# Eight blocks of an up projection made in two parts of the token columns

## Chip, cores and metric

The kernel runs on one core of a Trainium2 chip. Times are device microseconds of one execution; the time before is the median of two runs, 1305.54 us (1305.24 and 1305.84).

## What is computed

The reference is two transformer blocks over 256 tokens of width 1024, in float32. The first block mixes tokens (a gated branch and a banded attention) and then goes through a layer of 16384 experts, each with one up row and one down row. Every token picks 16 experts for each of 8 heads:

```python
q = (xb @ w_query).reshape(PEER_TOKEN_BLOCK, PEER_HEADS, 2, PEER_HALF)
...
g = jax.nn.softmax(best, axis=-1)
u = jnp.take(expert_u, eidx, axis=0)
h = jax.nn.gelu(jnp.einsum('thkd,td->thk', u, xb))
vv = jnp.take(expert_v, eidx, axis=0)
return jnp.einsum('thk,thkd->td', (g * h.astype(jnp.float32)).astype(xb.dtype), vv)
```

The second block has three mixers, gates, and a feed-forward layer of width 2816. The change concerns the product with `expert_u` only.

## The kernel before

The kernel doesn't gather experts. `experts` (L681) computes the up projection of all 16384 experts for all 256 tokens as 128 dense blocks of 128 experts, applies GELU, multiplies by a dense matrix of gates that is zero where a token didn't pick an expert, and computes the dense down projection in 128 blocks. The routing that makes the gates runs beside this on VectorE.

Every large product is made in three matmuls of the type float32r: each operand is held as a high part and a low part, and `mm3` (L179) adds high x high (L180), high weight x low (L181) and low weight x high (L182) into PSUM. The trace writes both float32r and plain float32 as f32. `project` (L187) does so for the 8 slices of the width 1024, so one block of the up projection is 24 matmuls of 128 rows by 256 token columns, with the 128 x 128 weight slices as the stationary operand; each matmul has its own weight load (LDWEIGHTS, the engine PEld in the trace). The token operands are the tiles `nh` and `nl`, the weights `wh` and `wl`:

```python
for k in range(n):
    wh, wl = self.cols(w, o + k)
    self.mm3(ps, wh, wl, xh[:, k0 + k, :], xl[:, k0 + k, :], k == 0, k == n - 1)
```

Weights come by DMA on SyncE's queue into `raw` (L166); ScalarE copies the high part (L171) and VectorE subtracts to make the low part (L116). Three blocks of weights are held ready at a time, and `ahead` (L104) starts the load of a later block when a buffer comes free.

The loop over the up blocks is at L754. Two blocks share one PSUM bank, `ps` (256 columns each), and after each odd block ScalarE applies GELU to both (L771). At i = 2, 22, 42 and 62 the loop first issues `short` (L257): four small f16 matmuls (L261). After each block `side.step` (L767) issues a share of VectorE's routing work: top-16 searches, one-hots and gates. The order of instructions on every engine is the order in which the program issues them.

Other lines that the text speaks of: L708 are plain float32 matmuls of 128 columns (the key scores of the routing); L229 are plain float32 matmuls of one column (mean squares for a norm); L846 and L870 are plain float32 matmuls of 256 columns; L669 are f16 matmuls of 64 columns (gates); L255 are matmuls on zeros of 128 columns, in plain float32, which the program issues at its start and later where TensorE would be idle.

Of the kernel before, what the change touches and what calls it, by code (L numbers as in the profile page):

```python
# [13 lines left out]
S = 256  # L14
# [41 lines left out]
class Prog:  # L56
# [624 lines left out]
    def experts(self):  # L681
        nc, tc, a, c = self.nc, self.tc, self.a, self.c
        with tc.tile_pool(name="sg", bufs=1) as sg:
# [19 lines left out]
            def scores(hp, qt):  # L703
                nonlocal pss
                if hp % 4 == 0:
                    pss = [self.bank("g").rearrange("p (h c) -> p h c", h=4) for _ in range(2)]
                for t in range(2):
                    self.mm(pss[t][:, hp % 4, :], qt[:, t * P:(t + 1) * P], sk[:, hp, :], start=True, stop=True)  # L708
                if hp % 4 == 3:
                    for t in range(2):  # L710
                        self.act(sc[t][:, hp - 3:hp + 1, :], pss[t], AF.Copy)
                    ready[0] += 1
# [3 lines left out]
            for hp in range(16):  # L716
# [6 lines left out]
                if hp < 2:  # L723
                    ps = first[hp]
                else:
                    ps = self.bank()[:, 0:S]
# [27 lines left out]
            for i in range(P):  # L754
                if i == 64:
                    side.rate = self.RATE[1]
                if i % 2 == 0:
                    ps = self.bank().rearrange("p (e t) -> p e t", e=2)
                if i in (2, 22, 42, 62):
                    self.short(iot)  # L760
                self.project(ps[:, i % 2, :], self.take(), self.nh, self.nl)
                while prev:
                    scores(*prev.pop(0))
                if i == P - 1:
                    side.rest()
                    self.hidden(hb0, hb1, 0)
                side.step()  # L767
                self.ahead()
                if i % 2:
                    o = self.up_order[i - 1]  # L770
                    self.act(hb0[:, o:o + 2, :] if i < 64 else hb1[:, o - 64:o - 62, :], ps, AF.Gelu_apprx_tanh)  # L771
# [38 lines left out]
            for i in range(P - 2):  # L810
# [4 lines left out]
                w = self.take()  # L815
# [26 lines left out]
            ps = self.pair()[:, 0, :].rearrange("p (e t) -> p e t", e=2)  # L842
            for j in range(2):
                w = self.take()
# [483 lines left out]
```

## Time and profile before

| what | value |
|---|---|
| median of two runs | 1305.54 us |
| the profiled execution | 1305.5 us |
| its span, first to last instruction | 1303.7 us |
| TensorE busy | 1291.5 us, 11518 matmuls |
| weight loads busy | 1256.1 us, 11518 loads |
| VectorE busy | 945.8 us |
| ScalarE busy | 673.0 us |
| granted TensorE clock | 0.999 of full speed |

Busy time counts each instruction from start to end, overlaps once. Matmuls overlap one another, so the pace of a run of matmuls is read from the starts, or from a run's length and count: (length - duration of the last) / (count - 1).

### The profile page before, as it was taken

To read this page: it belongs to the slowest core of one execution; us is meant where nothing else is said; L and a number is where in the kernel's file an instruction comes from. 1 tells how busy PE (TensorE), PEld (TensorE's weight loads), DVE (VectorE), ACT (ScalarE), POOL (GpSimd) and SP (SyncE) were. 2 spreads that over 40 slices of the span, in tenths; PEclk is the share of its full clock that TensorE was granted. 3 is DMA by queue.
4 is the path that set the end of the run, shared out by engine and by line. 5 is a ranking of instruction groups with operands and counts; after the bars stand their busy time and mean duration, and the time that the engine had idled before them with its cause. 6 is when DMAs were issued, how large, how long until landed. Compare 5 with 4: busy or idle time off the path is not lost.

```text
span 1303.7 us, 27324 instructions
## 1 busy us (share of the span) xinstructions
PE 1291.5 (99%) x11518; PEld 1256.1 (96%) x11518; DVE 945.8 (73%) x1517; ACT 673.0 (52%) x935; POOL 1.6 (0%) x9
## 2 busy tenths in 40 slices
PE   9999999999999999999999999999999999999998
PEld 8799999999999999999999999999999999999986
DVE  5567899878888887799985665556567576776743
ACT  7575454454544444444444554444677646655542
POOL 0000000000000000000000000000000000000000
PEclk9999999999999999999999999999999999999999
DMA  8545466655655555555556755564644456455652
GB/s 273 188 128 179 162 196 197 196 191 193 190 184 176 170 173 176 182 173 170 175 165 194 257 186 193 192 194 149 228 147 147 147 193 217 160 189 193 194 186 74
DMA packets 65211, 237.14 MB, mean 182 GB/s; under 512 B 7360, under 2 KB 7488, under 8 KB 64576
## 3 DMA queue, kind: packets, MB, share of 16 engines
q1 hardware_dynamic: 64800, 233.30, 54.8%
q10 hardware_dynamic: 288, 2.10, 0.5%
q8 instruction: 90, 1.47, 0.4%
q14 instruction: 33, 0.27, 0.1%
HBM read 233.27 MB, written 2.10 MB: 181 GB/s over the span
## 4 chain that ended last, share of the span: by engine, by line
PE 94%; DVE 3%; ACT 2%; issue 1%; DMA 1%; SPq 0%; DVEq 0%; ACTq 0%
PE u L180 20%; PE u L181 19%; PE u L182 19%; PE g L180 7%; PE g L181 7%; PE g L182 7%; PE y L180 3%; PE y L182 3%; PE y L181 3%; PE y L669 2%; DVE wl L116 1%; ACT wh L171 1%; PE y L870 1%; DMA raw<-w_in_t 1%; PE y L846 1%
## 5 line engine op out<-in xcount | busy, mean ns | idle before, releaser
L116 DVE TENSOR_TENSOR wl<-raw,wh 128x1024 fp32r<-128x1024 f32 x426 | 519.1, 1222 | 271.4 <-ACT wh L171 270.7
L171 ACT ACTIVATE wh<-raw 128x1024 fp32r<-128x1024 f32 x426 | 451.1, 1060 | 485.5 <-PE u L181 376.6
L180 PE MATMUL u<-nh,wh 128*128 128x256 f32 x2176 | 609.6, 280 | 0.2 <-ACT big L1017 0.2
L181 PE MATMUL u<-nl,wh 128*128 128x256 f32 x2176 | 602.4, 277 | 0.9 <-DVE nl L733 0.5
L182 PE MATMUL u<-nh,wl 128*128 128x256 f32 x2176 | 601.7, 277 | 0.7 <-DVE wl L116 0.7
L180 PEld LDWEIGHTS u<-nh,wh 128*128 128x128 f32 x2176 | 408.7, 188 | 2.8 <-issue 1.7
L181 PEld LDWEIGHTS u<-nl,wh 128*128 128x128 f32 x2176 | 408.9, 188 | 2.0 <-DVE nl L272 0.7
L182 PEld LDWEIGHTS u<-nh,wl 128*128 128x128 f32 x2176 | 408.5, 188 | 1.0 <-DVE wl L116 0.9
L180 PE MATMUL g<-nh,wh 128*128 128x256 f32 x680 | 188.2, 277 | 0.0
L182 PE MATMUL g<-nh,wl 128*128 128x256 f32 x680 | 187.8, 276 | 0.0
L181 PE MATMUL g<-nl,wh 128*128 128x256 f32 x680 | 187.8, 276 | 0.0
L180 PEld LDWEIGHTS g<-nh,wh 128*128 128x128 f32 x680 | 127.6, 188 | 0.3 <-issue 0.3
L182 PEld LDWEIGHTS g<-nh,wl 128*128 128x128 f32 x680 | 127.7, 188 | 0.0
L181 PEld LDWEIGHTS g<-nl,wh 128*128 128x128 f32 x680 | 127.7, 188 | 0.0
L658 DVE TENSOR_TENSOR og<-ob,gT 128x1024 f16<-128x1024 f16 x64 | 41.4, 688 | 1.1
L654 DVE TENSOR_TENSOR oa<-iot,i1T 128x2048 f16<-128x2048 f16 x32 | 39.0, 1218 | 0.0
L669 PE MATMUL y<-og,oa 128*128 128x64 f16 x1024 | 35.4, 193 | 0.0
L669 PEld LDWEIGHTS <-oa 128*128 128x128 f16 x1024 | 31.6, 98 | 1.1
L1017 ACT ACTIVATE big<-u 128x256 f32<-128x256 f32 x30 | 11.5, 383 | 27.2 <-PE u L182 27.2
L181 PE MATMUL y<-brl,wh 128*128 128x256 f32 x80 | 22.4, 280 | 0.0
L180 PE MATMUL y<-brh,wh 128*128 128x256 f32 x80 | 22.3, 279 | 0.0
L182 PE MATMUL y<-brh,wl 128*128 128x256 f32 x80 | 22.3, 279 | 0.0
(342 smaller groups left out, 1388.8 us busy)
## 6 DMA issues: line engine op xcount, KB each, us to landing
raw<-peer_u SPq DMA_DIRECT2D x128, 512.0 KB, 3.6
raw<-peer_v SPq DMA_DIRECT2D x128, 512.0 KB, 3.6
raw<-w_in_t SPq DMA_DIRECT2D x50, 512.0 KB, 3.9
raw<-ffn_in SPq DMA_DIRECT2D x44, 512.0 KB, 4.0
raw<-ffn_out SPq DMA_DIRECT2D x22, 512.0 KB, 3.5
raw<-w_out SPq DMA_DIRECT2D x16, 512.0 KB, 3.6
raw<-w_query SPq DMA_DIRECT2D x16, 512.0 KB, 3.5
raw<-w_in_v SPq DMA_DIRECT2D x12, 512.0 KB, 4.4
```

The lines of the kernel that those rows point to most:

```text
L116: self.tt(out=lo, in0=raw, in1=h.bitcast(F32), op=ALU.subtract)
L171: self.act(h, raw, AF.Copy)
L180: self.mm(ps, wh, xh, start=start, stop=False, **kw)
L181: self.mm(ps, wh, xl, start=False, stop=False, **kw)
L182: self.mm(ps, wl, xh, start=False, stop=stop, **kw)
L654: tt(out=split(oa), in0=row(0, P), in1=runs(i1T[:, d], P), op=ALU.is_equal)
L658: tt(out=split(og[:, s]), in0=split(ob), in1=runs(gT[:, s, d], 64), op=ALU.mult)
L669: nc.tensor.matmul(ps[:, j, :], oa[:, j, :], og[:, s, j, :], start=(s == 0), stop=(s == 1))
L846: self.mm(ps[:, j, :], w[:, k * P:(k + 1) * P], self.mem[:, k, :], start=(k == 0), stop=(k == KD - 1))
L870: mm(pss[:, t, 0:256], self.mem[:, 4 * i + k, t * P:(t + 1) * P], w[:, k * 256:(k + 1) * 256], start=(4 * i + k == 0), stop=(4 * i + k == ...
L1017: copy = lambda v, scale=1.0: lambda ps: act(v, ps, AF.Copy, scale=scale)
```

## The change

For i // 2 = 4, 5, 6 and 7 (blocks 8 to 15) the block's product is made in two calls of `project`, over the columns n to 256 and then over 0 to n, with n = 32, 48, 64 and 128. All other blocks have n = 0 and one call over 256 columns, as before.

```diff
-                self.project(ps[:, i % 2, :], self.take(), self.nh, self.nl)
+                n = {4: 32, 5: 48, 6: 64, 7: 128}.get(i // 2, 0)
+                w = self.take()
+                for o, m in ((n, S), (0, n)):
+                    if o < m:
+                        self.project(ps[:, i % 2, o:m], w, self.nh[:, :, o:m], self.nl[:, :, o:m])
```

On TensorE, where block 7 ends and block 8 begins, the order before is this (`u_2134` is the PSUM bank of blocks 6 and 7, `u_2206` that of 8 and 9; `wh_2129` and `wl_2130` are the weights of block 8):

```order
L180 MATMUL u_2134<-nh_74,wh_2094 128x256
L181 MATMUL u_2134<-nl_75,wh_2094 128x256
L182 MATMUL u_2134<-nh_74,wl_2095 128x256
L180 MATMUL u_2206<-nh_74,wh_2129 128x256
L181 MATMUL u_2206<-nl_75,wh_2129 128x256
L182 MATMUL u_2206<-nh_74,wl_2130 128x256
```

Now the same place reads so:

```order
L180 MATMUL u_2134<-nh_74,wh_2094 128x256
L181 MATMUL u_2134<-nl_75,wh_2094 128x256
L182 MATMUL u_2134<-nh_74,wl_2095 128x256
L180 MATMUL u_2206<-nh_74,wh_2129 128x224
L181 MATMUL u_2206<-nl_75,wh_2129 128x224
L182 MATMUL u_2206<-nh_74,wl_2130 128x224
```

The matmuls of block 8 have 224 columns instead of 256.

On TensorE 24 matmuls further, before, block 8 ends and block 9 (weights `wh_2166`, `wl_2167`) begins:

```order
L180 MATMUL u_2206<-nh_74,wh_2129 128x256
L181 MATMUL u_2206<-nl_75,wh_2129 128x256
L182 MATMUL u_2206<-nh_74,wl_2130 128x256
L180 MATMUL u_2206<-nh_74,wh_2166 128x256
L181 MATMUL u_2206<-nl_75,wh_2166 128x256
L182 MATMUL u_2206<-nh_74,wl_2167 128x256
```

Now block 8 goes on there with its second part:

```order
L180 MATMUL u_2206<-nh_74,wh_2129 128x224
L181 MATMUL u_2206<-nl_75,wh_2129 128x224
L182 MATMUL u_2206<-nh_74,wl_2130 128x224
L180 MATMUL u_2206<-nh_74,wh_2129 128x32
L181 MATMUL u_2206<-nl_75,wh_2129 128x32
L182 MATMUL u_2206<-nh_74,wl_2130 128x32
```

The 24 matmuls of 32 columns use the weights of block 8 a second time, in the same sequence; block 9 comes 24 matmuls later. TensorE has 192 matmuls more in all, and the other engines have the instructions that they had, in the same order.

## Rows read from the trace of the kernel before

**Rows 1.** The page: busy time by engine, and the chain by engine.
```profile
span 1303.7 us, 27324 instructions
PE 1291.5 (99%) x11518; PEld 1256.1 (96%) x11518; DVE 945.8 (73%) x1517; ACT 673.0 (52%) x935; POOL 1.6 (0%) x9
...
PE 94%; DVE 3%; ACT 2%; issue 1%; DMA 1%; SPq 0%; DVEq 0%; ACTq 0%
```

**Rows 2.** Timeline of PE around the short matmuls: start, length, engine, line, form, count.
```profile
171.80 0.29 PE L261 MATMUL y<-iot 128*128 128x64 f16 x4
171.92 0.36 PE L180 MATMUL u<-nh,wh 128*128 128x256 f32 x1
172.12 0.29 PE L181 MATMUL u<-nl,wh 128*128 128x256 f32 x1
...
226.43 0.29 PE L261 MATMUL y<-iot 128*128 128x64 f16 x4
226.56 0.36 PE L180 MATMUL u<-nh,wh 128*128 128x256 f32 x1
```

**Rows 3.** Windows: length, busy time of each engine, granted clock, DMA.
```profile
1.00:5.00 4.00, 3.98 (x19) 3.98 (x20) 0.71 (x2) 2.12 (x4) 0.00 (x0) 1.00 0.79 227
...
188.28:210.08 21.80, 21.80 (x195) 21.80 (x194) 21.21 (x75) 10.44 (x12) 0.00 (x0) 1.00 0.65 211
```

**Rows 4.** The chain in the window 188.28 to 210.08, by line.
```profile
by line: PE u L180 34.0%; PE u L181 33.7%; PE u L182 33.2%
```

**Rows 5.** Timeline of PE in the up blocks, first and last of 42 steps.
```profile
190.05 0.28 PE L180 MATMUL u<-nh,wh 128*128 128x256 f32 x1
190.16 0.28 PE L181 MATMUL u<-nl,wh 128*128 128x256 f32 x1
...
194.81 0.28 PE L180 MATMUL u<-nh,wh 128*128 128x256 f32 x1
```

**Rows 6.** Groups of instructions from 188 to 211 us: count, busy time, mean ns.
```profile
L180 PE MATMUL u<-nh,wh 128*128 128x256 f32 x68 | 18.8, 276 | 0.0
L180 PEld LDWEIGHTS u<-nh,wh 128*128 128x128 f32 x68 | 12.8, 188 | 0.0
```

**Rows 7.** L229 (ns min/median/max) and the timeline around it; L846's durations.
```profile
L229 PEld LDWEIGHTS y<-cst,big x28: 186/192/192, 124.4 to 1132.7; 128*128 128x128 f32 x28
L229 PE MATMUL y<-cst,big x28: 164/250/271, 124.4 to 1132.8; 128*128 128x1 f32 x28
...
904.09 1.37 PE L229 MATMUL y<-cst,big 128*128 128x1 f32 x11
...
900.50 3.61 PE L846 MATMUL y<-big,raw 128*128 128x256 f32 x16
903.95 1.84 PE L229 MATMUL y<-cst,big 128*128 128x1 f32 x16
905.66 3.70 PE L846 MATMUL y<-big,raw 128*128 128x256 f32 x16
...
L846 PE MATMUL y<-big,raw x32: 377/379/463, 900.5 to 909.0; 128*128 128x256 f32 x32
```

**Rows 8.** L708: its durations, and 12 of them in the timeline.
```profile
L708 PE MATMUL g<-hb x64: 270/275/275, 123.6 to 168.9; 128*128 128x128 f32 x64
...
167.71 1.50 PE L708 MATMUL g<-hb 128*128 128x128 f32 x12
```

**Rows 9.** L669: its durations, and 32 of them in the timeline.
```profile
L669 PEld LDWEIGHTS <-oa x1024: 95/98/101, 374.7 to 680.4; 128*128 128x128 f16 x171
L669 PE MATMUL y<-og,oa x1024: 193/193/203, 374.7 to 680.4; 128*128 128x64 f16 x171
...
374.72 1.11 PE L669 MATMUL y<-og,oa 128*128 128x64 f16 x32
```

**Rows 10.** Timeline of float32r matmuls of 512 columns.
```profile
56.42 0.40 PE L180 MATMUL u<-wh,nh 128*128 128x512 f32 x1
...
57.35 0.40 PE L181 MATMUL u<-wl,nh 128*128 128x512 f32 x1
```

**Rows 11.** Timeline of the last block of queries, first and last of 14 steps.
```profile
165.24 0.28 PE L180 MATMUL u<-nh,wh 128*128 128x256 f32 x1
...
166.89 0.28 PE L182 MATMUL u<-nh,wl 128*128 128x256 f32 x1
```

**Rows 12.** Timeline of the first matmuls of the run.
```profile
1.02 3.99 PE L255 MATMUL u<-zeros 128*128 128x128 f32 x17 [1.02 <-POOL zeros L248]
```

## Prediction

> **What bounds the kernel now.** I read the page first. TensorE is busy 1291.5 of 1303.7 us, and the chain that ended last is 94% PE [rows 1], so a stretch in which TensorE is slower moves the end, unless another engine waits there. Next comes the stretch that the change touches. The short matmuls at i = 2 and i = 22 place it: the first matmul behind them starts at 171.92 and 226.56, with 20 blocks and one more group of four short ones (0.13 us) between [rows 2]. That is (54.64 - 0.13) / 20 = 2.726 us a block, so blocks 8 to 15 stand from 171.92 + 6 x 2.726 = 188.28 to 210.08. In that window TensorE and its weight loads are busy for all of 21.80 us, VectorE for 21.21 [rows 3], and the chain runs through PE alone [rows 4]. VectorE is nearly full, but nothing there waits for it, and since the change only lengthens TensorE's part, VectorE gets more room.
>
> Then the pace of one matmul. A duration in the list (276 ns) overlaps the next one, so I take starts. From 190.05 to 194.81 there are 14 groups of three, 42 steps in 4.76 us: 113.3 ns for 256 columns [rows 5]. The weight loads keep the same pace, and their record of 188 ns shows the same overlap [rows 6]. So two things could set this pace, the 256 columns or the load of a 128x128 fp32 weight, and the change separates them: it halves the columns of a matmul on average and doubles the loads.
>
> **What the change removes and adds.** An up block is 8 x 3 = 24 matmuls. Eight blocks lose 192 matmuls of 256 columns: 192 x 113.3 ns = 21.75 us, which is the window of 21.80. They get 384 matmuls, each with its own load, since all 24 of the first part run before the second part begins and the weights change at each step. The number of columns is the same.
>
> What does a matmul cost that has few columns and a load of 128x128 fp32 weights? The trace has three witnesses. One column: 11 matmuls of the mean-square in 1.37 us, the last lasting 0.250, so (1.37 - 0.25) / 10 = 112.0 ns a step [rows 7]. 128 columns of plain fp32: 12 in 1.50 us, the last 0.275, so 111.4 [rows 8]. Against them 64 columns of f16: 32 in 1.11 us, the last 0.193, so 29.6 ns, and there the load is of f16 weights, with a record of 98 ns where the fp32 one has 188 to 192 [rows 6, 7, 9]. One column and 128 take the same time, and a change of the weights' type changes it: the load of fp32 weights sets some 112 ns, whatever the columns. I take 111.7, the mean of the two. The loads of the up projection are float32r, and they have the shape and the record length of the plain fp32 ones.
>
> Added: 384 x 111.7 = 42.89 us. Net: 42.89 - 21.75 = +21.1 us. By this all eight blocks come out alike, at 24 x 2 x 111.7 = 5.36 us in place of 2.72, whether cut 224 + 32 or 128 + 128.
>
> Bounds of this term. From below: a wide part could be paced by its columns if its load hid better than here. 512 columns step at (57.35 - 56.42) / 4 = 232.5 ns [rows 10], so a column costs (232.5 - 113.3) / 256 = 0.466 ns, and 224, 208 and 192 columns would take 98.4, 90.9 and 83.5. With the small part at 111.7 the pairs cost 96.8, 89.3 and 81.9 more than 113.3, and 128 + 128 costs 110.1 more: 48 of each make 18.2 us. From above: the same 256-column matmul also runs at (166.89 - 165.24) / 14 = 117.9 ns in a stretch just before [rows 11]; at that pace the parts take 45.3 us, and 16 changes of width could each cost what the first matmul behind the short ones does, 0.20 in place of 0.113 us [rows 2], 1.4 us in all. With blocks 16 to 21 at 117.9 until the next short group (144 x 4.6 ns = 0.7 us) that is 23.5 + 1.4 + 0.7 = 25.6 us. I take the middle, as rows 7 and 8 are loads of just this shape at full clock.
>
> The rest of the edit costs nothing. Other engines keep their instructions in number and order; semaphore waits stand on the first matmul that uses a buffer, as before. Weight buffers and the PSUM bank come free 2.6 us later per block, so loads, Copies and GELUs of these blocks move with TensorE. Their cover is TensorE's own work, now twice as long. Later waits of TensorE that slack could absorb are absent: its idle time in the whole run is 12.2 us [rows 1], and none of it lies in this stage [rows 3].
>
> A rule that speaks against the doubling stands in the Trainium skill, "TensorE: Matmul & The Clock Gate", section "Back-to-back issue gap": warm, a gap is N / 2.4 + 2.5 ns, and about 25 ns at least, a load not being counted. By it a pair of parts costs nearly what one matmul of 256 does, and the sum would be near zero instead of +21 us. Rows 9 fit that rule, and rows 7 and 8 do not, since their weights are fp32; here the measured step decides. What the rule would make of the time is the second rival.
>
> **Sum.** The profiled execution took 1305.5 us (span 1303.7 and 1.8 around it), and the median of the runs shown is 1305.54, so no correction is needed: 1305.5 + 21.1 = 1326.6 us, +1.6%. A measurement of this kernel tells about 2% (26 us) from no change, and the forecast stays inside that. Its own range is 1323.7 (+18.2) to 1331.1 (+25.6).
>
> **Rivals.**
>
> 1. Below 256 columns float32r loses its advantage and runs as plain fp32 does; this ends slower by more than 2%. Plain fp32 shows two records for each matmul of the program (32 for the 16 of L846), each (3.61 - 0.379) / 15 = 215.4 ns for 256 columns [rows 7]. In proportion two records cost 377, 350, 323 and 223 ns for 224, 208, 192 and 128, and two loads, 223, for each small part. Pairs: 600, 573, 546 and 446, less 113.3 each, 48 times: +82 us, 1388. It decides from the first split matmul on, and passes the 2% line if pairs cost over 249 ns on average. For it: no row here has float32r under 256 columns. Against it: float32r shows one record per matmul at both 256 and 512 columns, and its cost from 256 to 512 is nearly in proportion. 7%.
>
> 2. The load hides, and columns alone count. 256 columns at 113.3 scale to 99.1, 92.1, 85.0 and 56.7, with 29.6 as the least a small part takes (32, 48 and 64 columns): pairs of 128.7, 121.7, 114.6 and 113.4, 48 x 25.2 ns = +1.2 us, 1306.7. For it: rows 9. Against it: rows 7 and 8. 5%. That the split isn't made is excluded by the order of the instructions, which shows its rows.
>
> 3. TensorE's clock falls to its lower level. In the first matmuls of the run, of 128 columns and behind idle time, 17 stand in 3.99 us, some 0.23 us a step against 0.111 later [rows 8, 12]: these rows read as the 1.2 GHz level, though the granted clock is given as 1.00 there too [rows 3]. The Trainium skill, same page, "Part 1: The HAM clock gate", says that the clock starts low and that being busy releases it. If parts of 32, 48 and 64 columns count as too little work, each of the six blocks that have them could pay its 5.36 us again: +32 us more, 1359. Against it: a run of 16 one-column matmuls keeps its 112 ns throughout, and the plain fp32 behind it takes 3.70 us for 16, hardly more than the 3.61 ahead of it [rows 7]. 8%.
>
> **How the numbers follow.** Load-bound 80%, plain-fp32 pace 7%, hidden load 5%, clock 8%. Predicted: 1326.6. For 8 in 10 the range must reach past the likeliest case: up by one or two blocks at the low clock (5.4 us each), down a little below its own lower bound: 1320 to 1337. Faster by over 2%: 0.01. Slower by over 2%: 0.07 from the first rival, 0.08 from the third, of which a block or two alone stays near the line, 0.14 together. Within 2%: 0.85.
>
> **What would show it.** In the trace after, the stretch from 188.3 should be about 43 us long with TensorE busy throughout, starts 111 to 113 ns apart in every part, the weight loads at the same step, and blocks 16 onward at 113.3 again. VectorE's share there falls to about half. Wide parts with steps of 84 to 98 ns would mean the lower bound; steps near 30 ns in the small parts, the second rival; two records per matmul or steps that grow with the columns, up to 377 ns at 224, the first; steps of 0.23 us, the third. The forecast is wrong if the four cuts differ much from each other.

## The result, and the profile after

The changed kernel takes 1360.16 us (1359.57 and 1360.76) against 1305.54: 1.0415 times the time before, 95% interval 1.0396 to 1.0433. That is 54.6 us slower. The forecast was 1326.6 us, with a range up to 1337. The doubled loads cost what the working said; the rest is TensorE's clock, which the sum of the forecast held at full speed throughout.

The page of the changed kernel, busy time by engine and two of its rows by 40 slices; below them the same two rows of the page before:

```profile
span 1359.0 us, 27708 instructions
PE 1346.6 (99%) x11710; PEld 1311.4 (97%) x11710; DVE 947.2 (70%) x1517; ACT 673.1 (50%) x935; POOL 1.6 (0%) x9
...
PEclk9999995599999999999999999999999999999999
DMA  8535541156555555555555755555544455465662
...
PEclk9999999999999999999999999999999999999999
DMA  8545466655655555555556755564644456455652
```

TensorE's busy time is up by 55.1 us and VectorE's and ScalarE's by 1.4 and 0.1 [rows 1], so nearly all of the 55.3 us that the span grew lies on TensorE. Two slices of 34 us show a granted clock of five tenths. The DMA falls off there, to the 52 GB/s of the rows below: TensorE takes 10.25 us over a block's weights there, and new weights are loaded as it frees their buffers.

By stretch, in the same windows view as [rows 3] (length, busy time of PE, PEld, DVE, ACT, POOL, granted clock, DMA share, GB/s): block 8, block 9, then two blocks each of 208 + 48, 192 + 64 and 128 + 128, and the start of the first whole block:

```profile
188.70:194.07 5.37, 5.37 (x51) 5.37 (x49) 4.59 (x18) 1.56 (x3) 0.00 (x0) 0.98 0.65 214
194.07:201.19 7.12, 7.12 (x49) 7.12 (x50) 2.60 (x9) 1.05 (x2) 0.00 (x0) 0.74 0.29 104
201.19:221.67 20.48, 20.48 (x97) 20.48 (x98) 5.19 (x18) 2.59 (x3) 0.00 (x0) 0.50 0.16 52
221.67:242.15 20.48, 20.48 (x97) 20.48 (x98) 5.20 (x18) 2.60 (x3) 0.00 (x0) 0.50 0.15 52
242.15:262.67 20.52, 20.52 (x97) 20.52 (x98) 6.56 (x26) 2.60 (x3) 0.00 (x0) 0.50 0.15 52
262.67:265.60 2.93, 2.93 (x15) 2.93 (x16) 1.78 (x4) 1.54 (x2) 0.00 (x0) 0.51 0.00 0
```

Block 8 takes the 5.37 us that the sum gave it. Block 9 takes 7.12, and the last six 10.25 each, nearly twice the load-bound 5.36, at a clock of 0.50, the level of 1.2 GHz. The eight blocks take 73.97 us where they took 21.8. TensorE is busy in every microsecond of this: a busy share tells nothing here, and the granted clock tells all.

The timeline of PE shows the two mechanisms apart (start, length, engine, line, form, count):

```profile
191.14 0.27 PE L181 MATMUL u<-nl,wh 128*128 128x224 f32 x1
191.25 0.27 PE L182 MATMUL u<-nh,wl 128*128 128x224 f32 x1
...
191.40 0.26 PE L181 MATMUL u<-nl,wh 128*128 128x32 f32 x1
191.51 0.26 PE L182 MATMUL u<-nh,wl 128*128 128x32 f32 x1
...
194.40 0.41 PE L181 MATMUL u<-nl,wh 128*128 128x224 f32 x1
194.61 0.41 PE L182 MATMUL u<-nh,wl 128*128 128x224 f32 x1
...
197.34 0.27 PE L180 MATMUL u<-nh,wh 128*128 128x224 f32 x1
197.46 0.28 PE L181 MATMUL u<-nl,wh 128*128 128x224 f32 x1
...
200.62 0.31 PE L180 MATMUL u<-nh,wh 128*128 128x32 f32 x1
200.77 0.37 PE L181 MATMUL u<-nl,wh 128*128 128x32 f32 x1
200.98 0.37 PE L182 MATMUL u<-nh,wl 128*128 128x32 f32 x1
...
203.01 0.41 PE L182 MATMUL u<-nh,wl 128*128 128x208 f32 x1
203.22 0.41 PE L180 MATMUL u<-nh,wh 128*128 128x208 f32 x1
...
208.02 0.39 PE L182 MATMUL u<-nh,wl 128*128 128x48 f32 x1
208.23 0.39 PE L180 MATMUL u<-nh,wh 128*128 128x48 f32 x1
...
245.18 0.41 PE L182 MATMUL u<-nh,wl 128*128 128x128 f32 x1
245.39 0.41 PE L180 MATMUL u<-nh,wh 128*128 128x128 f32 x1
...
265.13 0.41 PE L182 MATMUL u<-nh,wl 128*128 128x256 f32 x1
265.34 0.38 PE L180 MATMUL u<-nh,wh 128*128 128x256 f32 x1
265.55 0.29 PE L181 MATMUL u<-nl,wh 128*128 128x256 f32 x1
265.68 0.28 PE L182 MATMUL u<-nh,wl 128*128 128x256 f32 x1
```

In block 8, 224 columns and 32 columns step alike, 0.11 us: the load sets the pace, as rows 7 and 8 said. As the first part of 32 columns ends, the step becomes 0.21. It goes back to 0.11 within block 9's wide part, is lost again at 200.8 as the second part of 32 ends, and now 208, 48 and 128 columns all step at 0.21 until whole blocks of 256 have run for 2.9 us. Steps of this kind, 0.21 us in place of 0.11, are what the prediction named as the sign of its third rival (there put at 0.23).

### The profile page after: what moved, and what is told of

Same layout as the page of the kernel before. It is cut to its first block, busy times and chain, and to the rows that moved or that the text cites. A ratio compares the mean times of both kernels' runs of the same rounds, so it can differ in the third digit from the quotient of the medians.

```text
span 1359.0 us, 27708 instructions
## 1 busy us (share of the span) xinstructions
PE 1346.6 (99%) x11710; PEld 1311.4 (97%) x11710; DVE 947.2 (70%) x1517; ACT 673.1 (50%) x935; POOL 1.6 (0%) x9
## 4 chain that ended last, share of the span: by engine, by line
PE 96%; ACT 2%; DVE 2%; DMA 1%; issue 0%; SPq 0%; DVEq 0%; ACTq 0%
PE u L180 20%; PE u L181 20%; PE u L182 20%; PE g L181 6%; PE g L180 6%; PE g L182 6%; PE y L180 3%; PE y L182 3%; PE y L181 3%; PE y L669 2%; ACT wh L171 1%; DMA raw<-w_in_t 1%; PE y L874 1%; PE y L850 1%; PE g L708 0%; DVE wl L116 0%
## 5 line engine op out<-in xcount | busy, mean ns | idle before, releaser
L180 PE MATMUL u<-nh,wh 128*128 128x256 f32 (+3 forms) x2240 | 641.4, 286 | 0.7 <-ACT wh L171 0.5
L181 PE MATMUL u<-nl,wh 128*128 128x256 f32 (+3 forms) x2240 | 633.7, 283 | 0.6 <-DVE nl L733 0.5
L182 PE MATMUL u<-nh,wl 128*128 128x256 f32 (+3 forms) x2240 | 633.4, 283 | 0.8 <-DVE wl L116 0.8
L180 PEld LDWEIGHTS u<-nh,wh 128*128 128x128 f32 x2240 | 436.6, 195 | 3.5 <-issue 1.7
L181 PEld LDWEIGHTS u<-nl,wh 128*128 128x128 f32 x2240 | 436.6, 195 | 1.3 <-DVE nl L733 0.7
L182 PEld LDWEIGHTS u<-nh,wl 128*128 128x128 f32 x2240 | 436.2, 195 | 1.1 <-DVE wl L116 1.0
L669 PE MATMUL y<-og,oa 128*128 128x64 f16 x1024 | 35.4, 193 | 0.0
L669 PEld LDWEIGHTS <-oa 128*128 128x128 f16 x1024 | 31.6, 98 | 1.1
```

The source lines that it names most:

```text
L180: self.mm(ps, wh, xh, start=start, stop=False, **kw)
L181: self.mm(ps, wh, xl, start=False, stop=False, **kw)
L182: self.mm(ps, wl, xh, start=False, stop=stop, **kw)
L669: nc.tensor.matmul(ps[:, j, :], oa[:, j, :], og[:, s, j, :], start=(s == 0), stop=(s == 1))
```

## The experiments

Theory A: the load costs 112 ns a matmul at full clock, and the clock falls only behind the narrow parts of 32, 48 and 64 columns. Theory B: doubling the loads is enough, so the clock falls with every cut and in every order. Runs 1 to 8 are single executions beside one of the kernel before (1305.18 us for the first four, 1305.93 for the next). The edits are shown against the changed kernel, those of runs 3 and 8 against the kernel before.

**Run 1: all eight blocks 128 + 128.**

```diff
-                n = {4: 32, 5: 48, 6: 64, 7: 128}.get(i // 2, 0)
+                n = 128 if 8 <= i < 16 else 0
```

> All eight blocks are cut 128 + 128. Theory A (stretches): the load of fp32 weights sets 112 ns a matmul, and the clock falls only where a stretch of some us has hardly any columns, as the parts of 32, 48 and 64; 128 columns a load keep it. Then steps of 112 ns throughout, clock full, eight blocks in 42.9 us, about 1326.6 us. Theory B (half): the clock falls wherever the columns fill only about half of the time that the loads take, on average over a block. Then steps of 213 ns after the first few us, eight blocks in about 80 us, about 1365 us.

Measured: 1326.79 us. The windows view of the eight blocks:

```profile
188.50:231.30 42.80, 42.80 (x386) 42.80 (x385) 24.15 (x89) 10.40 (x12) 0.00 (x0) 1.00 0.38 120
```

42.80 us for 384 matmuls is 111.5 ns each, at full clock. This is the forecast's sum without its miss: 42.9 us for the blocks and 21.6 us on the whole time, where 21.1 was expected. Theory B falls, and so do the forecast's first two rivals for this cut (446 and 113 ns a pair, where 42.80 / 192 is 223). Its lower bound, which is about the wide parts, falls with block 8 above: 224 columns step at 0.11 us, not at 0.098.

**Run 2: all eight blocks 224 + 32.**

```diff
-                n = {4: 32, 5: 48, 6: 64, 7: 128}.get(i // 2, 0)
+                n = 32 if 8 <= i < 16 else 0
```

> All eight blocks are cut 224 + 32. Theory A: the clock falls late in or after each part of 32 columns and is given back within each part of 224, as in the first two blocks of the changed kernel (second block 7.1 us): 5.4 + 7 x 7.1 = 55 us for the eight, about 1339 us. Theory B: an average of 128 columns a load, as in every other cut, so the clock stays low: about 1365 us.

Measured: 1339.76 us.

```profile
188.06:242.25 54.19, 54.19 (x387) 54.19 (x385) 24.15 (x89) 10.41 (x12) 0.00 (x0) 0.78 0.29 94
```

Same number of matmuls, loads and columns as run 1, 11.4 us more in these blocks, and a clock of 0.78: the distribution of the columns costs it, not their number. The parts of 224 take most of the price here: each but the first has 15 to 17 of its 24 matmuls at 0.21 us and the rest at 0.11.

**Run 3: wide and narrow matmul of each product behind one another.** The cuts of the changed kernel; one start flag for the bank, since both parts accumulate side by side.

```diff
-                self.project(ps[:, i % 2, :], self.take(), self.nh, self.nl)
+                n = {4: 32, 5: 48, 6: 64, 7: 128}.get(i // 2, 0)
+                w = self.take()
+                if n:
+                    for k in range(KD):
+                        wh, wl = self.cols(w, k)
+                        for e, (wt, xt) in enumerate(((wh, self.nh), (wh, self.nl), (wl, self.nh))):
+                            for o, m in ((n, S), (0, n)):
+                                self.mm(ps[:, i % 2, o:m], wt, xt[:, k, o:m], start=(k == 0 and e == 0 and o > 0),
+                                        stop=(k == KD - 1 and e == 2 and o == 0), skip_group_check=True)
+                else:
+                    self.project(ps[:, i % 2, :], w, self.nh, self.nl)
```

> The cuts of the changed kernel, but wide and narrow part of each of the 24 products directly behind one another, so no stretch has narrow matmuls alone; same number of matmuls, loads and columns. Theory A: steps of 112 ns throughout at full clock, about 1326.6 us. Theory B: low clock after the first few us, steps of 213 ns, about 1365 us.

Measured: 1326.23 us.

```profile
187.90:231.00 43.10, 43.10 (x388) 43.10 (x388) 24.20 (x89) 10.65 (x13) 0.00 (x0) 1.00 0.36 119
...
189.65 0.37 PE L768 MATMUL u<-nh,wl 128*128 128x224 f32 x2
189.88 0.38 PE L768 MATMUL u<-nh,wh 128*128 128x224 f32 x2
190.10 0.37 PE L768 MATMUL u<-nl,wh 128*128 128x224 f32 x2
```

The same 384 matmuls as in the changed kernel, in another order, and 34 us of its 55 are gone: the clock stays at 1.00 when each narrow matmul stands between wide ones. (A line of the view counts a wide and a narrow matmul together, x2.) A pair of matmuls on the same weights still takes 0.22 us (189.65, 189.88, 190.10), so the second load, which the program issues as before, is paid even where the weights are the ones just loaded.

**Run 4: the four cuts in the opposite order.**

```diff
-                n = {4: 32, 5: 48, 6: 64, 7: 128}.get(i // 2, 0)
+                n = {4: 128, 5: 64, 6: 48, 7: 32}.get(i // 2, 0)
```

> The same four cuts in the opposite order: two blocks of 128 + 128, then 192 + 64, 208 + 48, 224 + 32. Theory A: blocks 8 and 9 keep the clock (5.4 us each); it falls at the first part of 64 columns or soon after, the cuts 192 + 64 and 208 + 48 stay low (10.2 us each), 224 + 32 gets it back for a part (7 us each): about 1345 us. Theory B: it falls in block 8 and stays low: about 1365 us.

Measured: 1333.89 us, 11 us less than theory A's estimate. Pairs of blocks in order, 128, 64, 48, 32:

```profile
188.69:199.36 10.67, 10.67 (x98) 10.67 (x97) 7.29 (x27) 2.60 (x3) 0.00 (x0) 1.00 0.57 184
199.36:210.05 10.69, 10.69 (x98) 10.69 (x98) 5.20 (x18) 2.61 (x3) 0.00 (x0) 1.00 0.29 100
210.05:222.40 12.35, 12.35 (x99) 12.35 (x98) 5.20 (x18) 2.60 (x3) 0.00 (x0) 0.86 0.28 87
222.40:236.37 13.97, 13.97 (x98) 13.97 (x98) 6.56 (x26) 2.60 (x3) 0.00 (x0) 0.76 0.24 76
```

The parts of 64 columns keep the clock in this execution. It is lost three times, for 16 or 17 matmuls each, in the wide parts behind the parts of 48 and 32 (and a fourth time in the whole blocks behind), and every time it comes back within the same wide part, once one of 208 columns; the estimate had allowed for that with 224 only. So the 61 us that the last six blocks took in the changed kernel are not prices of those cuts; what went before matters. Runs 5 to 7 test that: theory H (history: 128 + 128 doesn't give a lost clock back) against P (each cut has its own price).

**Run 5: two blocks 224 + 32, then six of 128 + 128. Run 6: the same cuts, the six first.**

```diff
-                n = {4: 32, 5: 48, 6: 64, 7: 128}.get(i // 2, 0)
+                n = {4: 32, 5: 128, 6: 128, 7: 128}.get(i // 2, 0)
```

```diff
-                n = {4: 32, 5: 48, 6: 64, 7: 128}.get(i // 2, 0)
+                n = {4: 128, 5: 128, 6: 128, 7: 32}.get(i // 2, 0)
```

> Blocks 8 and 9 cut 224 + 32, blocks 10 to 15 cut 128 + 128. Theory H (history): the clock falls by the parts of 32 columns as in the changed kernel, and 128 + 128, which kept a full clock in the run with that cut alone, doesn't give a lost one back: blocks 8 and 9 12.5 us, six blocks of 10.25 us, about 1.5 us in the first whole blocks: about 1359 us. Theory P (each cut has its own price, whatever went before): six blocks of 5.4 us, about 1329 us.

> The same eight cuts in the opposite order: six blocks 128 + 128, then two of 224 + 32. Theories H and P alike: six blocks of 5.36 us, then 5.4 and 7.1, and 1.6 us in the blocks behind: about 1330 us. Under H the pair of runs differs by nearly 30 us, under P by nothing.

Measured: 1357.29 and 1327.59 us. Run 5, the two blocks of 224 + 32 and the six of 128 + 128; then run 6, all eight:

```profile
188.15:199.04 10.89, 10.89 (x98) 10.89 (x97) 7.20 (x27) 2.62 (x4) 0.00 (x0) 0.98 0.52 175
199.04:260.52 61.48, 61.48 (x289) 61.48 (x290) 16.96 (x62) 7.79 (x9) 0.00 (x0) 0.50 0.16 52
```

```profile
187.92:230.92 43.00, 43.00 (x387) 43.00 (x385) 24.16 (x89) 10.42 (x13) 0.00 (x0) 1.00 0.36 118
```

The same work in two orders differs by 29.7 us, as H said. In run 6, 128 + 128 runs at full clock throughout; in run 5 it is entered at the lower level and stays there for 61 us, until blocks of 256 follow. One thing was not as expected: in run 5 blocks 8 and 9 took 10.89 us and not 12.5. Up to there its matmuls are the same as those of the changed kernel, which took 5.37 + 7.12 = 12.49: the clock fell behind the first part of 32 columns there and not here. So cuts and order alone don't fix when it falls.

**Run 7: the changed kernel's order, with two whole blocks behind 224 + 32.**

```diff
-                n = {4: 32, 5: 48, 6: 64, 7: 128}.get(i // 2, 0)
+                n = {4: 32, 6: 48, 7: 64, 8: 128}.get(i // 2, 0)
```

> The four cuts of the changed kernel in its order, but with two whole blocks (10 and 11) behind the cut 224 + 32, the rest two blocks later. Theory H: the whole blocks give the clock back, so the cuts 208 + 48, 192 + 64 and 128 + 128 cost what they did in the opposite order, with a fall or two of 1.6 us: about 1333 us. Theory P: as the changed kernel, about 1360 us.

Measured: 1347.5 us, between H's 1333 and P's 1360. The two whole blocks, then the pairs of 48, 64 and 128, and below them matmuls near the start of the last pair:

```profile
200.71:207.88 7.17, 7.17 (x49) 7.17 (x50) 4.21 (x13) 2.58 (x3) 0.00 (x0) 0.78 0.23 75
207.88:220.15 12.27, 12.27 (x99) 12.27 (x97) 6.17 (x24) 2.60 (x3) 0.00 (x0) 0.86 0.40 128
220.15:234.12 13.97, 13.97 (x98) 13.97 (x98) 6.57 (x26) 2.60 (x3) 0.00 (x0) 0.76 0.25 77
234.12:254.19 20.07, 20.07 (x98) 20.07 (x98) 5.20 (x18) 2.60 (x3) 0.00 (x0) 0.51 0.16 53
...
234.49 0.28 PE L180 MATMUL u<-nh,wh 128*128 128x128 f32 x1
234.60 0.38 PE L181 MATMUL u<-nl,wh 128*128 128x128 f32 x1
234.77 0.42 PE L182 MATMUL u<-nh,wl 128*128 128x128 f32 x1
234.99 0.41 PE L180 MATMUL u<-nh,wh 128*128 128x128 f32 x1
```

The whole blocks give the clock back, and 208 + 48 and 192 + 64 cost 26.2 us where they had cost 41.0: H in kind. The miss is that 128 + 128, entered at full clock behind the last part of 64, lost it within half a microsecond (the steps go from 0.11 to 0.21) and then ran low to its end: 20.07 us against 10.67 in run 4.

**Run 8: small parts on f16 operands.** All eight blocks 224 + 32, the small part's 24 matmuls on a constant f16 tile; the product of those 32 columns is left out.

```diff
-                self.project(ps[:, i % 2, :], self.take(), self.nh, self.nl)
+                n = 32 if 8 <= i < 16 else 0
+                w = self.take()
+                self.project(ps[:, i % 2, n:S], w, self.nh[:, :, n:S], self.nl[:, :, n:S])
+                if n:
+                    for k in range(24):
+                        self.mm(ps[:, i % 2, 0:n], iot, iot[:, 0:n], start=(k == 0), stop=(k == 23))
```

> All eight blocks cut 224 + 32, with the 24 matmuls of the small part on f16 operands (a constant tile as weights and as columns): the product of the 32 columns of these blocks is left out. Load theory: the step is set by the load of the weights, 112 ns for fp32 and 30 for f16: 24 x (111.7 + 30) ns = 3.4 us a block and the clock kept, about 1311 us. If any matmul of few columns cost 112 ns: 5.36 us a block, 1326.6 us, and more with the clock.

Measured: 1312.59 us; the eight blocks, and one small part with the matmul behind it:

```profile
188.32:215.22 26.90, 26.90 (x387) 26.72 (x385) 22.77 (x82) 10.94 (x13) 0.00 (x0) 1.00 0.54 174
...
190.99 0.77 PE L766 MATMUL u<-iot 128*128 128x32 f16 x24
191.60 0.35 PE L180 MATMUL u<-nh,wh 128*128 128x224 f32 x1
```

24 matmuls start within 0.61 us, some 25 ns each, where the fp32 ones took 112, so the cost is not that of just any matmul with few columns. The edit changes the type of both operands, so by itself it doesn't say that the weights' load is what counts. A stretch of the kernel before, with plain fp32 weights of only 64 columns, does:

```profile
42.63 1.97 PE L440 MATMUL g<-cst,rqk 128*64 128x128 f32 x32
```

The last of these lasts 0.27 us, so the step is (1.97 - 0.27) / 31 = 55 ns: half the weights, half the step, with 128 columns of fp32 all the same. 26.90 us is 3.36 a block, close to the 3.4 expected. The clock stays at 1.00; whether because the narrow matmuls fill only 0.6 us and not 2.6, or because they are f16, this run doesn't tell.

**Runs 9 to 11: runs 7, 4 and 3 timed in rounds**, beside seven executions of the kernel before (1305.12 to 1306.33).

> The kernel of the run with two whole blocks behind the first cut, timed in rounds. If the falls of the clock depend on where the narrow parts happen to lie against the chip's own sampling, executions of the same kernel differ by several us, in steps of about 1.6 us for a fall that a wide part gives back, up to some 10 us where 128 + 128 runs low; if they are fixed by the kernel, executions agree within 0.3%, at 1347.5 us.

> The four cuts in the opposite order, timed in rounds. Chance of the moment: executions between about 1327 (no fall) and 1345 us. Fixed by the kernel: 1333.9 us within 0.3%.

> Wide and narrow part of each product directly behind one another, timed in rounds: no falls, so executions agree within 0.3% and the ratio to the kernel before is that of the doubled loads alone, (1305.5 + 21.1) / 1305.5 = 1.0162.

Measured, four executions each:

| kernel | us | ratio, interval | mean granted clock |
|---|---|---|---|
| two whole blocks between | 1346.1 to 1350.9 | 1.0331 (1.0314 to 1.0348) | 0.981 to 0.984 |
| opposite order | 1335.3 to 1341.8 | 1.0257 (1.0234 to 1.0281) | 0.987 to 0.992 |
| interleaved | 1326.0 to 1327.6 | 1.0160 (1.0143 to 1.0177) | 0.999 |

Where the clock falls, executions of one kernel spread by 4.8 and 6.5 us, and where it doesn't, by 1.6. The clock of each execution goes with its time (1335.3 at 0.992, 1341.8 at 0.987). The single numbers of runs 2, 4 and 7 are therefore good to some 5 to 7 us only; the 29.7 us between runs 5 and 6 are well beyond that. The kernel in the opposite order was profiled in run 4 and again in run 10. The two blocks of 208 + 48 in run 10:

```profile
209.48:223.46 13.98, 13.98 (x99) 13.98 (x98) 5.20 (x18) 2.60 (x3) 0.00 (x0) 0.76 0.24 76
```

In run 4 they took 12.35 us. In run 10 the clock fell once more, behind the second part of 64 columns: the same program, one fall more, 1.6 us. The interleaved kernel has the ratio expected of the doubled loads alone, 1.0162.

## Why the prediction was wrong

- **What bounds the kernel, and the blocks' place: right.** TensorE sets the end, nothing absorbs its added time, and the other engines cost nothing.
- **The load term: right, and now measured.** 111.7 ns a matmul was taken from fp32 rows; run 1 shows 111.5 in float32r, and the net of 21.1 us is 21.6 in run 1, 21.1 in run 3. The cuts cost the same at full clock (block 8 of the changed kernel 5.37 us, two blocks of 128 + 128 or of 192 + 64 in run 4 10.67 and 10.69, all four cuts in run 3 43.1). The f16 matmuls of run 8 step at some 25 ns, the fp32 ones at 111.5. The issue-gap rule of the Trainium skill ("TensorE: Matmul & The Clock Gate", "Back-to-back issue gap"), by which the sum would be near zero, fits the first and not the second; as that section says itself, it leaves the weight load out.
- **The first two rivals: wrong.** Neither do narrower matmuls take more than the load's time, nor does the load hide.
- **The step that failed: the sum has no term for the clock.** It takes all 384 matmuls at full clock and leaves a fall to the third rival, at 8%, and to one or two blocks in its upper bound. The runs show 32.6 us in its place: 31.2 in the eight blocks and 1.4 behind them. "Against it" stood one witness: 16 one-column matmuls that kept their pace and were followed by plain fp32 at full clock [rows 7]. That stretch lasted 1.84 us and stood between matmuls of 256 columns; a part of 32 lasts 2.6 us, and eight blocks of cut matmuls follow one another. Even a stretch like the new one would have been a weak witness: in run 5 the first part of 32 columns kept the clock and the second lost it. The records show no gap (7.12 us busy in a stretch of 7.12), and the clock fell all the same. The Trainium skill, same page, "Part 1: The HAM clock gate", puts the lower level down to idle time and its release to activity; no run here shows what the chip counts as either.
- **The third rival: right in kind, and near in its total by luck.** It charged each of the six blocks that have a narrow part 5.36 us, on its own: +32, 1359, where 1360.2 was measured. In fact block 8, one of the six, paid nothing; a fall that a wide part gives back costs some 15 to 17 x (213 - 112) ns, 1.5 to 1.7 us; and one that nothing gives back costs 10.25 - 5.36 = 4.9 us for every further block, 128 + 128 among them, though that cut has no narrow part. Six blocks did run low, those from block 10 on, but they are not the six that it named.

The account of the profiled execution: the eight blocks at full clock (42.80 in run 1) are 21.0 us over the window before; the low clock adds 73.97 - 42.80 = 31.2, and the first whole block behind it 14 x 0.1 = 1.4. That is 53.6 of the 55.3 us. Most of the other 1.7 is the pace of whole blocks elsewhere, and not this change: block 8 starts 0.3 us later than before, and from 779 to 812 us some 280 matmuls of 256 columns take 32.97 us where they took 31.75, at the two paces of [rows 5] and [rows 11].

What stays open: what exactly the chip counts. The same parts were followed by a fall in one execution and not in another (the first part of 32 in the changed kernel and in run 5, the second part of 64 in runs 10 and 4), so the program alone does not settle it; what else does, no run here shows. Nor does any show why a wide part gives a lost clock back in one run (208 columns in runs 4 and 10) and not in another (all of 208 and 192 in the changed kernel).

No version beat the kernel before. The best form of this change is the interleaved one, at 1.016.

## What to carry to other kernels

A matmul on 128 x 128 weights in fp32 or float32r took 112 ns here at full clock, however few its columns, and one of 256 columns took 113; so cutting a product of 256 columns in two doubled its time whatever the cut. Narrow matmuls of that kind, 24 in a row for 2.6 us, cost TensorE half its clock sooner or later in every run that had them, while its busy share read 100%; between wide ones (run 3) they did not. What follows them decides the price: whole blocks of 256 columns gave the clock back every time, wide parts of 192 to 224 sometimes, 128 + 128 never. Before a change that thins out TensorE's columns, look for a stretch in the trace that is as thin for as long as the new one will be, and if there is none, give the clock a large share of the chances.

## What was not expected of the hardware

What went before counts: 128 + 128 stepped at 111.5 ns for 32 us in run 6, where it was entered at full clock, and at 213.5 for 61 us in run 5, where it was entered at the lower level. It is not proof against a fall, though: in run 7 it was entered at full clock behind a part of 64 and lost it at once. At the lower level the load-bound step itself nearly doubles (213 ns for 48, 128 and 208 columns alike, where it was 112), and 256 columns step at 0.21 us too, so being bound by loads is no shelter from the lower clock. At the start of the run the granted clock reads 1.00 while the steps are 0.23 us [rows 3, 12]; for the stretches inside the run it agreed with the steps.
